# Log-softmax backward: rows dealt to partitions so that the 16 transfer engines walk neighbouring 64 KiB runs

## The chip, the cores and the metric

One core of a Trainium2 chip; the chip's other cores are idle. The metric is device time in microseconds (us), the median of several executions. The time of an experiment without a count of runs is that of its one execution. TensorE is not used.

## The reference

```python
# y, dy: (8, 1024, 8192) float32, y is a log-softmax over the last axis
softmax_x = np.exp(y)
sum_dy = np.sum(dy, axis=-1, keepdims=True)
return dy - softmax_x * sum_dy
```

There are 8192 independent rows of 32 KiB. All of y and dy must be read and a third array of that size written: 3 x 268.4 MB = 805.3 MB.

## The kernel before

A group is 256 rows: each of the 128 partitions holds a pair of consecutive rows, 64 KiB. There are 32 groups, worked on in twos. All transfers are issued from SyncE's queue.

```python
R = 2;  W = R * D;  G = N // (P * R)          # D = 8192, P = 128, W = 16384 floats = 64 KiB, G = 32
y_v   = y.flatten_outer_dims().rearrange("(g p r) d -> g p (r d)", p=P, r=R)     # dy_v, out_v alike
x_ts  = [pool.tile([P, W], fp32, name=f"x{j}") for j in range(2)]
y_t   = pool.tile([P, W], fp32, name="y_t")

def load_dy(g, x):      nc.sync.dma_start(out=x[:], in_=dy_v[g])
def load_y(g, lo, hi):  nc.sync.dma_start(out=y_t[:, lo:hi], in_=y_v[g][:, lo:hi])

for g in range(0, G, 2):
    load_dy(g, x_ts[0]);      load_y(g, 0, W)
    ...                       # row sums of dy on VectorE and ScalarE; exp(y); x += exp(y) * (-sum)
    load_dy(g + 1, x_ts[1])
    ...
    for r in range(R):
        load_y(g + 1, r * D, (r + 1) * D)     # two half-size y loads
        ...
    for j in range(2):
        nc.sync.dma_start(out=out_v[g + j], in_=x_ts[j][:])
```

So a period (two groups) is seven transfers: dy, y, dy, half y, half y, out, out.

Of the kernel before, what the change touches and what calls it, by code (L numbers as in the profile page):

```python
# [1 line left out]

# [5 lines left out]


EXP = mybir.ActivationFunctionType.Exp  # L10
COPY = mybir.ActivationFunctionType.Copy
ALU = mybir.AluOpType


@with_exitstack
def kernel(
    ctx: ExitStack,
    tc: tile.TileContext,
    y: bass.AP,
    dy: bass.AP,  # L20
    out: bass.AP,
):




    nc = tc.nc
    P = nc.NUM_PARTITIONS
    fp32 = mybir.dt.float32

    N, D = y.flatten_outer_dims().shape
    R = 2
    W = R * D
    G = N // (P * R)
    assert N == G * P * R and D == 8192 and G % 2 == 0
    H = D // 2

    PIECES = [(0, 2048), (2048, 5120), (5120, D)]

    y_v = y.flatten_outer_dims().rearrange("(g p r) d -> g p (r d)", p=P, r=R)  # L40
    dy_v = dy.flatten_outer_dims().rearrange("(g p r) d -> g p (r d)", p=P, r=R)
    out_v = out.flatten_outer_dims().rearrange("(g p r) d -> g p (r d)", p=P, r=R)

    pool = ctx.enter_context(tc.tile_pool(name="pool", bufs=1))
    stats = ctx.enter_context(tc.tile_pool(name="stats", bufs=3))
    psum = ctx.enter_context(tc.tile_pool(name="psum", bufs=1, space=bass.MemoryType.PSUM))
    x_ts = [pool.tile([P, W], fp32, name=f"x{j}") for j in range(2)]
    y_t = pool.tile([P, W], fp32, name="y_t")
    copied = psum.tile([P, H], fp32, name="copied")

    def load_dy(g, x):
        nc.sync.dma_start(out=x[:], in_=dy_v[g])  # L52

    def sums(x):
        s_t = stats.tile([P, R], fp32, name="s_t")
        half_t = stats.tile([P, 2], fp32, name="half_t")
        nc.vector.tensor_reduce(  # L57
            out=s_t[:, 0:1], in_=x[:, :D], axis=mybir.AxisListType.X, op=ALU.add, negate=True
        )
        for h in range(2):  # L60
            nc.scalar.activation(  # L61
                copied[:], x[:, D + h * H : D + (h + 1) * H], COPY, accum_out=half_t[:, h : h + 1]
            )
        nc.vector.tensor_scalar(  # L64
            out=s_t[:, 1:2],
            in0=half_t[:, 0:1],
            scalar1=half_t[:, 1:2],
            scalar2=-1.0,
            op0=ALU.add,
            op1=ALU.mult,  # L70
        )
        return s_t

    def load_y(g, lo, hi):
        nc.sync.dma_start(out=y_t[:, lo:hi], in_=y_v[g][:, lo:hi])  # L75

    def compute(x, s_t, r):
        for b, e in PIECES:
            cs = slice(r * D + b, r * D + e)
            nc.scalar.activation(y_t[:, cs], y_t[:, cs], EXP)  # L80
            nc.vector.scalar_tensor_tensor(  # L81
                out=x[:, cs],
                in0=y_t[:, cs],
                scalar=s_t[:, r : r + 1],
                in1=x[:, cs],
                op0=ALU.mult,
                op1=ALU.add,
            )

    for g in range(0, G, 2):  # L90
        load_dy(g, x_ts[0])
        load_y(g, 0, W)
        s_t = sums(x_ts[0])
        for r in range(R):
            compute(x_ts[0], s_t, r)
        load_dy(g + 1, x_ts[1])
        s_t = sums(x_ts[1])
        for r in range(R):
            load_y(g + 1, r * D, (r + 1) * D)
            compute(x_ts[1], s_t, r)  # L100
        for j in range(2):
            nc.sync.dma_start(out=out_v[g + j], in_=x_ts[j][:])


# [1 line left out]
_INS = ['y', 'dy']  # L106
_OUTS = [((8, 1024, 8192), 'float32')]


# [23 lines left out]
```

## Time and profile before

| | before |
|---|---|
| time, median | 1867.6 us |
| transfer engines busy | 99.9% of the span |
| rate over the span | 432 GB/s |
| 64 KiB packet, median | 2.418 us (27.1 GB/s per engine) |
| VectorE, ScalarE busy | 860, 699 us |

The lines that carry this are in the prediction. Two lines of the issue table belong to them; the last figure is the median time from the issue of a transfer to its landing, and the first one is the half-size y load.

```profile
y_t<-in_y_dram SPq DMA_DIRECT2D x32, 4096.0 KB, 18.1
x<-in_dy_dram SPq DMA_DIRECT2D x32, 48.3
```

### The profile page before, as it was taken

How to read it: one execution, taken by the hardware profiler on the slowest of the kernel's cores; microseconds unless marked ns; L12 is line 12 of the kernel's file. 1: busy time of each engine (PE TensorE's matmuls, PEld its weight loads, DVE VectorE, ACT ScalarE, POOL GpSimd, SP SyncE). 2: the span in 40 equal slices, each digit the busy share in tenths (PEclk: the TensorE clock that was granted, in tenths of full speed). 3: DMA queues.
4: the chain of work that ended last, by engine and by line, in shares of the span. 5: the costliest groups of instructions: out<-in, count | busy, mean ns of one | idle time of the engine just before them, and what ended most of it. 6: DMA issues, size and time to landing. Idle time of an engine off the chain costs nothing.

```text
span 1865.9 us, 923 instructions
## 1 busy us (share of the span) xinstructions
DVE 859.8 (46%) x256; ACT 698.7 (37%) x321; POOL 0.2 (0%) x4
## 2 busy tenths in 40 slices
DVE  2907429074290732807328073280632806338063
ACT  2606326063260532605336052360523605236052
POOL 0000000000000000000000000000000000000000
DMA  9999999999999999999999999999999999999999
GB/s 427 424 430 427 430 447 427 427 431 445 427 427 441 426 437 434 438 431 427 437 438 429 433 428 440 434 431 437 425 438 436 433 436 425 439 433 436 434 428 391
DMA packets 16135, 805.37 MB, mean 432 GB/s; under 512 B 1792, under 2 KB 1792, under 8 KB 1792
## 3 DMA queue, kind: packets, MB, share of 16 engines
q1 hardware_dynamic: 16128, 805.31, 99.9%
q14 instruction: 7, 0.06, 0.0%
HBM read 536.87 MB, written 268.44 MB: 432 GB/s over the span
## 4 chain that ended last, share of the span: by engine, by line
DMA 64%; DVE 13%; ACT 10%; another core or an unknown queue 9%; issue 1%; SPq 0%; DVEq 0%; ACTq 0%
DMA x<-in_dy_dram 31%; DMA out_dram<-x 30%; DVE x L81 13%; ACT copied L61 6%; ACT y_t L80 4%; DMA y_t<-in_y_dram 3%; SPq L75 0%; DVEq L128 0%; ACTq L128 0%; SPq L52 0%; ACTq L80 0%; ACTq L61 0%
## 5 line engine op out<-in xcount | busy, mean ns | idle before, releaser
L81 DVE SCALAR_TENSOR_TENSOR x<-y_t,s_t,x 128x3072 f32<-128x3072 f32 (+1 forms) x192 | 579.4, 3059 | 255.7 <-ACT y_t L80 255.7
L57 DVE TENSOR_REDUCE s_t<-x 128x1 f32<-128x8192 f32 x32 | 277.8, 8682 | 722.3 <-DMA x<-in_dy_dram 722.3
L80 ACT ACTIVATE y_t<-y_t 128x3072 f32<-128x3072 f32 (+1 forms) x192 | 460.1, 2466 | 269.4 <-DMA y_t<-in_y_dram 253.2
L61 ACT ACTIVATE copied<-x 128x4096 f32<-128x4096 f32 x64 | 229.6, 3587 | 864.9 <-DMA x<-in_dy_dram 863.9
L61 ACT ACTIVATION_READ_ACCUMULATOR copied<-x 128x1 f32 x64 | 11.9, 186 | 0.0
L64 DVE TENSOR_SCALAR s_t<-half_t 128x1 f32<-128x1 f32 x32 | 6.5, 204 | 0.0
L61 ACT ACT_TABLE_LOAD x1 | 1.3, 1283 | 0.7 <-PEq L117 0.7
L117 POOL MEMSET const-bfloat16-1.0<- 128x1 bf16 x1 | 0.1, 101 | 0.0
L117 POOL MEMSET const-uint8-127<- 128x1 uint8 x1 | 0.1, 101 | 0.0
L117 POOL MEMSET const-float32-0.0<- 128x1 f32 x1 | 0.1, 98 | 0.2 <-issue 0.2
L117 POOL MEMSET const-float32-1.0<- 128x1 f32 x1 | 0.1, 98 | 0.0
## 6 DMA issues: line engine op xcount, KB each, us to landing
y_t<-in_y_dram SPq DMA_DIRECT2D x32, 4096.0 KB, 18.1
x<-in_dy_dram SPq DMA_DIRECT2D x32, 48.3
out_dram<-x SPq DMA_DIRECT2D x32, 32.5
y_t<-in_y_dram SPq DMA_DIRECT2D x16, 57.6
```

The lines of the kernel that those rows point to most:

```text
L57: nc.vector.tensor_reduce(out=s_t[:, 0:1], in_=x[:, :D], axis=mybir.AxisListType.X, op=ALU.add, negate=True)
L61: nc.scalar.activation(copied[:], x[:, D + h * H : D + (h + 1) * H], COPY, accum_out=half_t[:, h : h + 1])
L64: nc.vector.tensor_scalar(out=s_t[:, 1:2], in0=half_t[:, 0:1], scalar1=half_t[:, 1:2], scalar2=-1.0, op0=ALU.add, op1=ALU.mult,)
L80: nc.scalar.activation(y_t[:, cs], y_t[:, cs], EXP)
L81: nc.vector.scalar_tensor_tensor(out=x[:, cs], in0=y_t[:, cs], scalar=s_t[:, r : r + 1], in1=x[:, cs], op0=ALU.mult, op1=ALU.add,)
L117: nc = _bacc.Bacc("TRN2", target_bir_lowering=False, num_devices=1)
```

## The change

Intent: while all engines read at once, they should read memory that lies together. Row pairs are dealt out so that partition e*8+b of a group holds row pair b*16+e. If engine e owns partitions 8e to 8e+7, then at each step b the 16 engines stand in 16 neighbouring runs of 64 KiB.

```diff
-    y_v = y.flatten_outer_dims().rearrange("(g p r) d -> g p (r d)", p=P, r=R)
-    ... dy_v, out_v alike
+    E = 16
+    B = P // E
+    def view(t):
+        return t.flatten_outer_dims().rearrange("(g b e r) d -> g e b (r d)", b=B, e=E, r=R)
+    y_v, dy_v, out_v = view(y), view(dy), view(out)
...
-        nc.sync.dma_start(out=y_t[:, lo:hi], in_=y_v[g][:, lo:hi])
+        nc.sync.dma_start(out=split(y_t[:, lo:hi]), in_=y_v[g][:, :, lo:hi])     # split(t) returns t
```

The tile side of every transfer still counts 128 partitions. The DRAM side counts 16 (step 64 KiB) by 8 (step 1 MiB) in place of 128 (step 64 KiB).

More of the change, by code (lines that the diff above doesn't have):

```diff
@@ L38, with split @@
     PIECES = [(0, 2048), (2048, 5120), (5120, D)]
-    y_v = y.flatten_outer_dims().rearrange("(g p r) d -> g p (r d)", p=P, r=R)
-    dy_v = dy.flatten_outer_dims().rearrange("(g p r) d -> g p (r d)", p=P, r=R)
-    out_v = out.flatten_outer_dims().rearrange("(g p r) d -> g p (r d)", p=P, r=R)
+    E = 16
+    B = P // E
+    def view(t):
+        return t.flatten_outer_dims().rearrange("(g b e r) d -> g e b (r d)", b=B, e=E, r=R)
+    def split(t):
+        return t
+    y_v, dy_v, out_v = view(y), view(dy), view(out)
     pool = ctx.enter_context(tc.tile_pool(name="pool", bufs=1))
@@ L51, in load_dy @@
     def load_dy(g, x):
-        nc.sync.dma_start(out=x[:], in_=dy_v[g])
+        nc.sync.dma_start(out=split(x[:]), in_=dy_v[g])
     def sums(x):
@@ L101 @@
         for j in range(2):
-            nc.sync.dma_start(out=out_v[g + j], in_=x_ts[j][:])
+            nc.sync.dma_start(out=out_v[g + j], in_=split(x_ts[j][:]))
 _INS = ['y', 'dy']
```

## The prediction

The prediction supposes that the new shape deals the partitions to the engines in another way, and that engines then slow each other, two by two. That was the author's estimate; no trace had shown it. Its ways: A, they do not; B, they do until some are far enough ahead of the others; C, they do throughout; F, the new order of addresses is slow in HBM. The times of B and of C are estimates; C's factor of 1.75 to 1.95 is worked out from the spread of the completion writes of before, 0.65 and 3.8 us, on that supposition.

> **What bounds the kernel now.** I read the page of the profile first: its busy times, its slices, its queue table, its chain that ended last.
>
> ```profile
> span 1865.9 us, 923 instructions
> DVE 859.8 (46%) x256; ACT 698.7 (37%) x321; POOL 0.2 (0%) x4
> ...
> DMA  9999999999999999999999999999999999999999
> ...
> DMA packets 16135, 805.37 MB, mean 432 GB/s; under 512 B 1792, under 2 KB 1792, under 8 KB 1792
> ...
> q1 hardware_dynamic: 16128, 805.31, 99.9%
> ...
> DMA 64%; DVE 13%; ACT 10%; another core or an unknown queue 9%; issue 1%; SPq 0%; DVEq 0%; ACTq 0%
> ```
>
> VectorE works 46% of the span and ScalarE 37%, but the 16 transfer engines are busy in every slice and for 99.9% of the span. The chain of waits gives VectorE and ScalarE 23% between them; that is misleading, since a transfer queued earlier runs below every one of those steps. So the kernel ends when its 805.31 MB have gone through. The only question is at what rate, so I next took the view of chosen stretches, each two or four rows of data packets long, one with stores alone and two with loads alone:
>
> ```profile
> core 0: us, DVE busy (x) ACT busy (x) POOL busy (x), PEclk, DMA share, GB/s
> 81.50:100.83 19.33, 10.12 (x4) 7.22 (x3) 0.00 (x0) 1.00 1.00 434
> 121.20:140.53 19.33, 0.72 (x1) 0.67 (x1) 0.00 (x0) 1.00 1.00 434
> 120.50:159.15 38.65, 8.81 (x2) 7.42 (x4) 0.00 (x0) 1.00 1.00 434
> ```
>
> Stores (first row) and loads (the others) move 434 GB/s alike, whether VectorE is half busy or nearly idle. Per engine that is 434/16 = 27.1 GB/s. The trace's packet records say the same without averaging: of the 10240 packets of 64 KiB, the fastest took 2418 ns, the median 2418 ns, the 95th percentile 2422 ns, the mean 2420.1 ns; the 4096 packets of 32 KiB (the split y loads) have a floor of 1211 ns and a mean of 1226. Those numbers have no tail to speak of[...].
>
> **What could be won.** If every packet ran at its floor: (10240 x 2418 + 4096 x 1211) ns / 16 = 1857.5 us, against (10240 x 2420.1 + 4096 x 1226.0) / 16 = 1862.7 us now. So an HBM order that were perfect would win 5.2 us, 0.3%. "Faster by over 2%" would need packets shorter than any of the 10240 seen.
>
> [...]
>
> **The change part by part.** I built both programs and compared their instructions. DVE, ACT and POOL have the same instructions in the same order, and the SyncE queue has the same 112 transfers with the same waits: 32 dy loads, 16 whole and 32 half y loads, 32 stores. Removed: nothing. Added: nothing. The rows are computed independently and the stores use the same permutation as the loads, so the result is right. Descriptors stay runs of 64 KiB or 32 KiB, one per partition, so still 14336 data packets. What moves is the shape of the DRAM side: before it counts 128 (step 64 KiB); after, it counts 16 (step 64 KiB) by 8 (step 1 MiB), while the SBUF side counts 128.
>
> That has two effects.
>
> First, on HBM: [...] Worth 0 to -5 us by the sum above.
>
> Second, and this is where I put the result: on the split. [...]
>
> How far in step are they? In before, the 16 completion writes of the first load lie within 0.65 us, and of the last store within 3.8 us[...]. With fair sharing, a lead of d in a half of length 9.67 us (four packets) saves d of the doubling: the half lasts (2 x 9.67 - d). With d = 0.65 the factor is 1.93, with d = 3.8 it is 1.61; [...]I take 1.75 to 1.95, i.e. 1863 x 1.75 = 3260 to 1863 x 1.95 = 3630 us. I choose 1.85 for this way: 3450 us. The compute is no bound there: VectorE's 860 us lie under it.
>
> **The rivals.**
> A[...]. For it: nothing but the time budget is known here, and the change's author expected a gain. [...] Time: 1862 to 1872 us. I give it 17%.
> B, conflict that undoes itself[...]. [...]a dy load lands a median 48.3 us after its issue, so 2.5 transfers of 19.3 us are in line. [...]2180 us, and up to 2500[...]. 25%.
> C, engines in step, as worked out: 3260 to 3700. 45%.
> D, something between B and C (2500 to 3260), 11%.
> E, HBM order helps by more than the floor permits: 2%; it contradicts the packet floor.
> F, [...] Nothing in before speaks for it (every run is long), and it would look like C in time but differ in that loads and stores need not be hit alike. Counted inside C and D.
>
> **Range and chances.** A: 17%, B 25%, D 11%, C 45%, E 2%. The middle of this mass lies a little under C's lower end; I put the prediction between it and C's own figure, 3300 us, because C is the single likeliest way. A range without A holds 81%: 1960 to 3720 us. Faster by over 2%: 0.02; within 2%: 0.17; slower by over 2%: 0.81.
>
> **What would show it right or wrong.** If C: the queue table still shows 16128 packets and near 100% busy, with about 230 GB/s; 64 KiB packets take about 4.5 us instead of 2.42, in loads and stores alike; VectorE's and ScalarE's busy times stay 860 and 699 us and their idle times grow. If B: packets of two kinds, 2.42 us and up to 4.84 us, the long ones getting fewer, and completion writes of one transfer spread over about 10 us. If A: every line as before. If F: loads slow and stores not, or the other way round. I am wrong at the step "the split changes" if 64 KiB packets stay at 2.42 us throughout[...], and wrong only in the size of the drift if packets are a mixture.

## The result

| | before | changed |
|---|---|---|
| time, median | 1867.6 us | 3615.2 us (3601.8 to 3627.4, 4 runs) |
| 64 KiB packet, median | 2.418 us | 5.019 us |
| 32 KiB packet, median | 1.214 us | 2.454 us |

The ratio is 1.936, with a 95% interval of 1.929 to 1.943. (Ratios are the mean time of one kernel's fast runs over that of the other's in the same rounds, so not quite the ratio of the quoted medians.) The packet figures are from the trace's transfer records. The page of the changed kernel, the lines that answer to those of before:

```profile
span 3625.6 us, 923 instructions
DVE 861.3 (24%) x256; ACT 698.7 (19%) x321; POOL 0.2 (0%) x4
...
DMA packets 16135, 805.37 MB, mean 222 GB/s; under 512 B 1792, under 2 KB 1792, under 8 KB 1792
...
q1 hardware_dynamic: 16128, 805.31, 99.3%
...
another core or an unknown queue 61%; DMA 22%; ACT 12%; DVE 3%; issue 0%; ACTq 0%; DVEq 0%
...
y_t<-in_y_dram SPq DMA_DIRECT2D x32, 4096.0 KB, 52.6
x<-in_dy_dram SPq DMA_DIRECT2D x32, 100.0
```

Same instructions, packets and bytes, same busy time on VectorE and ScalarE, and transfer engines that are still busy for 99% of a span almost twice as long. So they did not wait for work; each packet took longer. "Busy" hides this: only the rate (222 against 432 GB/s) shows it. The chain of waits is of no use here: its 61% of "another core or an unknown queue" cannot be another core, since there is none; it is time that the view could not put down to a transfer.

Then chosen stretches of the changed kernel: one load, the first store, the second store, and loads later on. The last two figures are the transfer engines' busy share and GB/s. This view counts a packet whole where it starts, so a share can come out a little over 1.00.

```profile
44.00:84.60 40.60, 8.81 (x2) 7.42 (x4) 0.00 (x0) 1.00 1.00 207
165.00:198.00 33.00, 9.10 (x3) 7.22 (x3) 0.00 (x0) 1.00 0.99 232
198.50:236.00 37.50, 0.00 (x0) 0.00 (x0) 0.00 (x0) 1.00 0.97 218
960.00:1000.00 40.00, 8.05 (x2) 7.29 (x5) 0.00 (x0) 1.00 1.00 208
```

Before, the stretches shown read 434. Loads are at 207 in the first stretch and 208 in the last, stores a little better. To see single packets I strung the transfer records into 16 engines, each packet following the end of the one before (the records carry no engine number, so a few links can be wrong). The first transfers, mean over the engines, in ns:

```
changed, first dy load     4961 5127 5117 5120 | 4943 5120 5118 5116     sum 40.6 us
changed, first y load      4925 5119 5123 5114 | 4935 5114 5124 5115         40.6
changed, first half y      2366 2561 2564 2551 | 2375 2562 2555 2556         20.1
changed, first store       2588 2418 4795 5101 | 4345 5076 5075 4894         34.3
changed, second store      4123 5060 5060 4697 | 3958 5045 5044 4607         37.6
before, any whole transfer (8 x 64 KiB)                                      19.3
```

### The profile page after: what moved, and what is told of

It reads as the page before. It is cut to its first block, busy times and chain, and to the rows that moved or that the text cites. A ratio compares the mean times of both kernels' runs of the same rounds, so it can differ in the third digit from the quotient of the medians.

```text
span 3625.6 us, 923 instructions
## 1 busy us (share of the span) xinstructions
DVE 861.3 (24%) x256; ACT 698.7 (19%) x321; POOL 0.2 (0%) x4
## 3 DMA queue, kind: packets, MB, share of 16 engines
q1 hardware_dynamic: 16128, 805.31, 99.3%
## 4 chain that ended last, share of the span: by engine, by line
another core or an unknown queue 61%; DMA 22%; ACT 12%; DVE 3%; issue 0%; ACTq 0%; DVEq 0%
DMA y_t<-in_y_dram 21%; ACT y_t L89 8%; ACT copied L70 3%; DVE x L90 3%; DMA x<-in_dy_dram 1%; DVEq L137 0%; ACTq L137 0%; ACTq L89 0%; ACTq L70 0%
```

## The experiments

Theory P (partitions): it matters on which partitions the 16 engines stand at a time; on some sets of partitions they slow each other, and the 16 x 8 shape brings them onto such sets. This is a supposition, which the runs below test. Rival H (HBM): neighbouring runs, or steps of 1 MiB and more, collide in HBM. Rival S: the shape or the split costs time in itself, whatever the partitions.

### Same idea in the shape 32 x 4

```diff
-    E = 16
+    E = 32
```

> The change's idea with 32 x 4 in place of 16 x 8: partition e*4+b holds row pair b*32+e. [...]the DRAM side's slowest dimension is 32, each of its indices is four partitions[...]. Theory P[...]: 1862 to 1872 us, all 64 KiB packets near 2.42 us. Theory H (HBM: neighbouring runs or steps of 1 MiB and more collide): like the changed kernel, 3300 to 3700 us, or at least over 2000. Five rounds, because if P holds this run also tells whether the intended HBM order is worth anything: at most 5 us, 0.3%, by the packet floor.

Measured: 1866.37 us (1866.24 to 1866.77, 5 runs) against 1867.19, ratio 0.9993, interval 0.998 to 1.0007. A store and two loads of this run:

```profile
81.50:100.83 19.33, 10.76 (x4) 7.22 (x3) 0.00 (x0) 1.00 1.00 434
121.20:140.53 19.33, 0.26 (x1) 0.20 (x1) 0.00 (x0) 1.00 1.00 434
```

Full rate, 64 KiB packets of 2.418 us. Neighbouring runs and steps of even 2 MiB on the DRAM side (32 by 4) cost nothing here: 434 GB/s. And an HBM order of the intended kind, now without the other effect, is worth nothing that five rounds can see. (Whether the engines stand in sixteen neighbouring runs at a time, here or in the changed kernel, is not shown.)

### The shape 16 x 8 with another order on HBM, and its control in 32 x 4

```diff
-        return t.flatten_outer_dims().rearrange("(g b e r) d -> g e b (r d)", b=B, e=E, r=R)
+        v = t.flatten_outer_dims().rearrange("(q e j b r) d -> q j e b (r d)", j=2, b=B, e=E, r=R)
+        return [v[g // 2][g % 2] for g in range(G)]        # control: the same with E = 32
```

> The changed kernel's shape 16 x 8[...], but another order on HBM: the step of b is 64 KiB[...]. P: 3500 to 3700 us, load packets of 64 KiB near 5.0 us. H (if neighbouring runs are the cause): 1870 us, packets 2.42 us. If H is about the 1 MiB pitch instead, this one is slow too, and the next run tells.

> Control for the run before it: 32 x 4 with contiguous runs (256 KiB per index, 512 KiB apart)[...]. P: 1862 to 1872 us. H by 1 MiB pitch: slow where the 16 x 8 form is slow, over 2000 us.

Measured: 3579.1 us in 16 x 8, 1867.7 us in 32 x 4. Contiguous runs do not help 16 x 8, and do not hurt 32 x 4. In these four kernels the time follows the shape, and H would need a separate reason for each of the two slow orders. What closes it comes below: a run with the changed kernel's own HBM order that starts fast, and a pair with one HBM order and two speeds.

### Loads alone and stores alone in the shape of the change

```diff
 loads alone:   out_v as in before; y_v, dy_v = view(y), view(dy)
 stores alone:  y_v, dy_v as in before; out_v = view(out)
```

Both write wrong rows on purpose.

> The changed kernel's loads with the stores of before (the output rows come out permuted: a wrong result on purpose). In the changed kernel a group of four 64 KiB load packets took 20.1 us against 9.67 before. P: loads 537 MB at 217 GB/s x (9.67x2/20.1) = 2580 us, stores 268 MB at 434 = 618 us, in all about 3200 us (3050 to 3300). H gives the same, so this run sizes the loads' share and does not choose between the two; it would contradict both if under 2500 or over 3400.

> The changed kernel's stores with the loads of before (output rows permuted: a wrong result on purpose). The loads-only run took 3185 us, that is 1318 us over before. If the two shares add up to the changed kernel's 3615 - 1868 = 1747 us, the stores alone cost about 430 us: 2300 us. If stores were hit as hard as loads (20.1 us for four packets in place of 9.67), their 618 us would become 1285: 2530 us. Theory P[...] permits both[...].

Measured: 3185 us and 2421 us. The loads cost 1318 us over before, on 537 MB that took about 1237 us at 434 GB/s: 2.07 times as long. The stores cost 553 us on 618: 1.89 times. The second figure fell between the two that I had written down. Added up they give 1871 us, 124 more than the whole change's 1747, so together they cost a little less than apart. A load and a store of the loads-only run, then a store of the stores-only run:

```profile
44.00:84.60 40.60, 8.81 (x2) 7.42 (x4) 0.00 (x0) 1.00 1.00 207
165.00:200.00 35.00, 9.10 (x3) 7.22 (x3) 0.00 (x0) 1.00 0.98 425
```

```profile
82.00:117.00 35.00, 9.54 (x4) 6.67 (x3) 0.00 (x0) 1.00 0.99 212
```

### The changed kernel with engines started apart

```diff
+    lead = y.flatten_outer_dims().rearrange("(a c b r) d -> c a b (r d)", c=2, b=4, r=R)[0]
+    nc.sync.dma_start(out=x_ts[1][104:120, :], in_=lead[12:16])      # 16 packets of 64 KiB
+    nc.sync.dma_start(out=x_ts[1][40:88, :], in_=lead[0:12])         # 48 packets of 64 KiB
     for g in range(0, G, 2):
```

> The changed kernel, with two extra transfers in front (16 and 48 partitions, 4 MB in all, into a tile that is loaded again later)[...]. [...] P: the first dy and y loads then run at 2.42 us a packet although shape, split and HBM order are the changed kernel's; as long as the lead lasts the kernel runs near full rate. If sharing is fair and the lead is kept: about 2200 us; if the lead is lost in the half-size y loads or in the stores: a fast start and then the changed kernel's pace, up to 3600 us. A theory in which the split, the descriptors or HBM are slow in themselves: 5 us packets from the start, 3640 us.

The two transfers in front were meant to make some engines start four packets later than others.

Measured: 3564.9 us. The same stretch, first in the changed kernel, then in this run, then a later stretch of this run:

```profile
45.00:120.00 75.00, 26.23 (x8) 21.14 (x10) 0.00 (x0) 1.00 1.02 210
```

```profile
45.00:120.00 75.00, 26.82 (x8) 21.74 (x10) 0.00 (x0) 1.00 0.97 313
220.00:320.00 100.00, 26.41 (x8) 21.74 (x10) 0.00 (x0) 1.00 0.97 207
```

The shape and the HBM order are the changed kernel's, and yet it starts at 313 GB/s. One engine's packets in its first y load: 2759, 2422, 2422, 4202, then 2745, 2419, 2426, 4168 ns. Three of four packets take what a packet took before (2.418 us) or a little more, and one 4.2 us: the four take 11.8 us, against 9.67 before and 20.3 in the changed kernel's first y load. (The two transfers in front did not give quite the lead that was meant: some packets there took 7.3 us, three times 2.42.)

How the lead was lost can be read in two shorter stretches of this run:

```profile
100.00:107.00 7.00, 6.70 (x3) 7.00 (x4) 0.00 (x0) 1.00 0.77 309
111.00:116.00 5.00, 5.00 (x2) 0.00 (x0) 0.00 (x0) 1.00 1.01 210
```

In the first, by the packet records, four of the 16 engines are idle (hence the share of 0.77): they had finished the second dy load at 99.6 us, and the first half-size y load was issued only at 107.7 us, when VectorE had read the half of the y tile that it overwrites. Twelve engines then start that load together at 109 us, and the rate is down to 210. So those that were ahead lost their lead because their queue ran dry for some 9 us. Whether the lead would also have been lost in the half-size y loads themselves, with the queue full, is not shown. The stretch of the two stores that follow (150 to 220 us) still ran at 291 GB/s; the loads from 220 us on run at the changed kernel's pace, and in all this run is 50 us shorter. Neither S nor H can explain a fast start; P does.

### One number changed: where the tile lies

A program without compute: it copies dy to the output and loads y for nothing, in tiles of 64 partitions, DRAM side 16 x 4. P supposes that engines slow each other on partitions 0 to 63, and not on 32 to 95. The term exp(y) * sum is missing, which the comparison does not see.

```diff
-    LO = 0
+    LO = 32
     nc.sync.dma_start(out=x_ts[t % 3][LO : LO + 64, :], in_=dy_v[t])      # y load, store alike
```

> Transfers alone, no compute (a wrong result on purpose: it copies dy to the output and loads y for nothing): the same 805 MB in tiles of 64 partitions by 32 KiB, DRAM side 16 x 4[...], placed on partitions 0 to 63. [...] P: at most 217 GB/s, 3700 to 3900 us, 32 KiB packets of 2.42 us or more, also in the stores.

> The same program with one number changed: the tiles lie on partitions 32 to 95 in place of 0 to 63. Shape, split, HBM order, packets and count of partitions are the same[...]. P: near full rate, 1860 to 2000 us, 32 KiB packets near 1.21 us. If the split by shape or the HBM order were slow in itself, or if 64 partitions were: as slow as the run on partitions 0 to 63.

Measured: 3158.7 us on partitions 0 to 63, 2017.9 us on 32 to 95. A thousand microseconds from the middle of the first, and of the second:

```profile
500.00:1500.00 1000.00, 0.00 (x0) 1.00 0.99 257
```

```profile
500.00:1500.00 1000.00, 0.00 (x0) 1.00 1.00 401
```

Moving the tile by 32 partitions and nothing else makes 401 GB/s of 257. H and S are out as the cause of the slow one, since both are the same in the two. But both numbers miss what P expected. On 0 to 63 the early load packets took 2.56 us as expected, and the early store packets 1.21 us, as if stores did not slow each other; over the whole run 35% of the packets took under 1.5 us, and a third of all packets are stores. And on 32 to 95, 11% of the packets took over 1.5 us, which no run here explains; the first transfers, loads alone, ran at 1.213.

### Loads and stores in separate phases, 16 partitions a transfer

The fast stores suggested theory W, again a supposition: the partitions slow loads as P has it, and stores less: in the second of the placements below not at all, in the fourth half as much as loads. To take transitions and leads out, this program first loads 268 MB, then stores 268 MB, in transfers of 16 partitions by 32 KiB.

```diff
+    def part(j):
+        return x_ts[j][LO : LO + 15 * STEP + 1 : STEP, :]       # LO, STEP = 32, 4 | 0, 4 | 0, 8 | 0, 1
+    for t in range(T):
+        nc.sync.dma_start(out=part(t % 6), in_=dy_v[t])         # dy_v, out_v: "(t e) d -> t e d", e=16
+    for t in range(T):
+        nc.sync.dma_start(out=out_v[t], in_=part(t % 6))
```

> Loads and stores apart, no compute (a wrong result on purpose: only dy is read and some rows of it written everywhere): first 268 MB of loads, then 268 MB of stores, in transfers of 16 partitions by 32 KiB[...]. Here on partitions 32, 36, ... 92[...]. Both phases near 1.21 us a packet, 620 us each if the queue keeps up, about 1240 to 1400 us in all. It is the control of the next three.

> The same on partitions 0, 4, ... 60[...]. The copy on partitions 0 to 63 took 2.56 us for a load packet and 1.21 for a store packet. Theory W[...]: loads 2.4 to 2.6 us, stores 1.21 us: 1250 + 620 = 1870 us. Theory P as predicted[...]: 2.5 us in both, 2500 us.

> The same on partitions 0, 8, ... 120[...]. W: loads 2.4 to 2.6 us[...], stores too[...]: 2450 to 2650 us. If stores are free[...] and the changed kernel's stores were slowed by HBM: stores 1.21 us, 1870 us.

> The same on partitions 0 to 15[...]. W: loads 4.8 to 5.2 us[...], stores 2.4 to 2.6 us[...]: 2560 + 1280 = 3800 us. If reads too are limited[...]: also 2.4 to 2.6 us, but then the run on every eighth partition would show stores of 1.21.

| partitions | total us | load packet, mean ns | store packet, mean ns | loads, stores, GB/s |
|---|---|---|---|---|
| 32, 36, ... 92 | 1270.5 | 1217 | 1228 | 431, 421 |
| 0, 4, ... 60 | 2635.6 | 2564 | 2550 | 204, 204 |
| 0, 8, ... 120 | 2635.7 | 2564 | 2553 | 204, 204 |
| 0, 1, ... 15 | 5094.0 | 4814 | 5092 | 109, 102 |

The first two of these, a stretch of loads and a stretch of stores each:

```profile
100.00:600.00 500.00, 0.00 (x0) 1.00 1.00 431
700.00:1200.00 500.00, 0.00 (x0) 1.00 0.99 421
```

```profile
100.00:600.00 500.00, 0.00 (x0) 1.00 1.01 204
1400.00:2500.00 1100.00, 0.00 (x0) 1.00 1.00 204
```

W falls: it wanted stores of 1.21 us in the second row and of 2.5 us in the fourth. What remains is P in its plain form. In these four placements, which differ in nothing but the partitions, the packet time follows the placement, in both directions: 1.22 to 1.23 us, 2.55 to 2.56 us in two of them, and 4.8 to 5.1 us. By what rule the partitions belong together is not shown.

Why then were stores on 0 to 63 fast in the copy program? There each engine's store is 128 KiB and is queued right behind loads; in the changed kernel, too, the first two store packets after a load, again 128 KiB, took 2.59 and 2.42 us before the pace fell to 4.8 (table under "The result"). In the two-phase program the first stores wait for the last loads to land, and on 0, 4, ... 60 all but 9 of 8192 store packets took over 2 us. In the stores-only run, whose loads run at full rate (424 GB/s from 44 to 59 us), each engine's first store packet took 2.42 us, and its second already 4.2 to 4.8. Why the first packets are fast no run shows; it stays open.

## Why the prediction was right

**The bound.** Right: the transfers set the end (the three stretches shown for it are one or two whole transfers, eight or sixteen packets per engine, which the prediction calls rows), and VectorE's and ScalarE's busy times stayed at 861.3 and 698.7 us.

**What could be won.** Right: 5.2 us at most by the packet floor. The 32 x 4 run, which has an order of the intended kind at full rate, won 0.8 us of medians, with an interval that holds zero.

**The split changes.** Not contradicted by any run, and not seen: it was the author's estimate, and the records name no engine. What the runs show is that 16 x 8 is slow (3615.2 and 3579.1 us) and 32 x 4 fast (1866.4 and 1867.7 us) in two HBM orders each, and that the placement runs, which within a program differ in nothing but the partitions, took 3158.7 or 2017.9 us, and 1270.5 to 5094.0 us. In the changed kernel the first and the fifth packet of a load are some 0.2 us shorter than the rest (4.93 against 5.12 us in the first y load); why is not shown.

**Engines halve each other: up to 3700 us.** Right in kind as to the rate, with the size a little off; which engines slow which, no run shows. Half of the 434 GB/s of before is 217; loads ran at 207 in the changed kernel, and loads and stores at 204 in two of the placements, 5 to 6% less. For the load of 19.33 us that made 40.6, a factor of 2.10, where I had allowed at most 1.95.

**The relief by drift: 1.75 to 1.95, chosen 1.85.** Wrong as a mechanism, and lucky in the sum. In loads there was no relief: 207 GB/s at 44 us and 208 at 960 us, although the 16 completion writes of one transfer spread from 1.0 us at the start to 23 us after two periods and at times over 30 us later. So the engines drifted, but, to judge by the unchanged rate, not in a way that helped. The first two stores took 34.3 and 37.6 us, factors of 1.77 and 1.95, the range that I had named for all transfers. But the first store gained in its first two packets, and on engines that stood within some 1 us of each other: that is not drift but the fast start of stores, which stays open above. What gained the second store its smaller part is not shown. A doubling that cost more than I had allowed (2.10), and a gain in stores that I had not foreseen, offset each other: that 1.936 on the whole lies inside 1.75 to 1.95 is luck.

**The weights, and 3300 us.** The measured 3615 lies in my way C (3260 to 3700) and 15 us under its upper end for the changed kernel, 3630. The point was lower because I mixed in rival B at 25% and D at 11%. (With D's 11% spread evenly, the middle of the weights as listed is some 2900 us, not a little under C's lower end of 3260.) Half of B is real: engines that start apart do run faster, at 313 GB/s against 210 in the same stretch. The other half, that such a lead grows by itself, no run shows: in the changed kernel it never built up in loads, and one made by hand was lost when the queue ran dry. A and E, the rivals without a slowdown, and F, the HBM one, are refuted by the runs above.

**What would show it.** I had said 230 GB/s and packets of 4.5 us for C, and got 222 and 5.02 us for the median packet, with 4.65 us for the mean. "In loads and stores alike" missed the fast first packets of the stores. The wide spread of completion writes that I had named as a sign of B came, without B's gain.

## What to carry to other kernels

A rearranged view of a DRAM tensor can change more than addresses: in these runs its outermost count decided the rate. Where a permutation of a 128-partition tile is wanted, an outermost count of 32 or 128 kept full rate here (434 GB/s) and 16 halved it (207 in loads; others were not tried); read the rate, not the busy share (99.3% in the changed kernel), to see whether the engines slow each other. And look at the packet floor first: here nearly every packet already took 2.418 us, so no order of addresses had more than 5.2 us to win.
